# Two key blocks projected in the MLP's accumulation banks, and the first query group's rotations split between VectorE and GpSimd

## The chip, the cores and the metric

The kernel runs on one core of a Trainium2 chip, as one program. The metric is device time in microseconds, lower is better. A core has five engines that run side by side, each through its own list of instructions in order: TensorE (PE in the profile; its weight loads stand apart as PEld), VectorE (DVE), ScalarE (ACT), GpSimd (POOL), and SyncE (SP), which only issues transfers. They wait for one another through semaphores. Matmuls write into PSUM, which has eight banks here, each 128 rows by 512 float32 numbers; the other engines empty the banks.

## The reference

A trunk of two layers on 512 tokens of width 1024, in float32. Layer A is attention and a squared-ReLU MLP. Then keys and values are projected once, for all of layer B, whose attention reads them. Cut to what the change touches:

```python
for layer in range(DEPTH):
    h = rmsnorm(x, attn_norm[layer])
    ...
    else:                                                    # layer B
        k_s, v_s = jnp.split(rmsnorm(x, kv_norm) @ w_kv_shared, 2, axis=-1)
        k_shared = rope(rmsnorm(split_heads(k_s, DIL_SLOTS), kv_k_norm), pos)
        v_shared = split_heads(v_s, DIL_SLOTS)
        q, q_mem = jnp.split(h @ b_w_in[i], [B_Q], axis=-1)
        o_main = dilated_attention(q, k_shared, v_shared, b_q_norm[i])   # q: rmsnorm, rope
        o_mem = memory_attention(...)
        x = x + jnp.concatenate([o_main, o_mem], axis=-1) @ b_w_out[i]
    x = x + squared_relu_mlp(rmsnorm(x, mlp_norm[layer]), w_up[layer], w_down[layer])
```

`rope` turns each pair of halves (x1, x2) of a head into (x1 cos - x2 sin, x1 sin + x2 cos).

## The kernel before, in words

Every float32 product is made from two parts: a number is split into a rounded part and a remainder, and `mm3` (L260, L261, L262) issues three matmuls for each tile: rounded by rounded, rounded by remainder, remainder by rounded. A weight tile is loaded by SyncE into a staging tile `st` (three buffers), ScalarE writes the rounded part into a tile `w` (four buffers, L253), and VectorE or GpSimd subtracts for the remainder (L255; `lo="gv"` takes them by turns).

`proj` multiplies the tokens, in four blocks of 128, with a weight matrix. For each block it takes a bank from `pool` and runs over eight tiles k of the width, so a block has 24 matmuls. `order` is the order of the blocks. The function `evac` then empties the bank. A list as `pool` gives each block, by its number, a pool of its own:

```python
ps = self.ps(pool[b] if isinstance(pool, list) else pool or self.pacc, [P, n])
```

The PSUM pools are `pacc` (2 banks, tiles named `s_acc`), `pS` (3, `s_ps`), `pT` (2, `s_pt`) and `pO` (1, `s_po`).

The place of the first edit is the seam between the first MLP and layer B. The last quarter of the MLP accumulates in banks of all pools; `X` (two banks of `pacc`) and `V` (two of `pT`) are its last. VectorE adds a finished bank into the rows `xn` (L216, in `into`); the function `columns` then transposes 128 x 128 pieces of `xn` by TensorE into `pS` banks (L1251), copies them out (L1258 on ScalarE, L1256 on VectorE) and makes the gained copies (`gained`, L276 on ScalarE and L277 on VectorE) that are the stationary tiles `s_act` of the projections. The tokens of rows 1 (blocks 2 and 3) are ready before those of rows 0 (blocks 0 and 1), and in the last steps `into(X, 0, 0)` comes before the product into `V` has been added.

`layer_b` then projects the keys (`w_kv[0]`, `evac_k`), the values (`w_kv[1]`, `evac_v`), and, sharing TensorE with other work, the queries of four slot groups `sp` (`proj_b`). `evac_k` works on halves of a block: the square sums (`normf`, L505 to L514), a product with the gain that reads the bank (L1419), the rotation (`rope`, L524 to L527, on GpSimd) and a scaling (L1423, GpSimd). `evac_v` scales a block into a tile `raw` (two buffers, L1404) and GpSimd's queue stores it to memory (L1405). `proj_b` empties each block through `normf`, L1466, `rope`, a scaling (L746 in `q_out`), and the split into two parts (`hilo`, L697 on ScalarE, L698 on VectorE), after which TensorE transposes it (L755). `rope` takes its scratch from a tile `rb` with one buffer, whichever engine runs it, and `tq`, which holds the rotated block, has two.

The instructions of each engine are put into an order by a scheduler when the program is built, so an edit can move instructions far from its line. Line numbers after `proj_b`'s edit are two or three higher in the changed kernel (L1466 becomes L1468).

Of the kernel before, what the change touches and what calls it, by code (L numbers as in the profile page):

```python
# [14 lines left out]
P = 128  # L15
# [18 lines left out]
def bcast(ap, dim, n):  # L34

    a = [list(x) for x in ap.ap]
    a.insert(dim, [0, n])
    return bass.AP(tensor=ap.tensor, offset=ap.offset, ap=a)
# [30 lines left out]
def drain(*gens):  # L69
    for g in gens:  # L70
        for _ in g:
            pass
# [7 lines left out]
def weave(main, fill, ratio):  # L80

    due, fill = 0.0, iter(fill)
    for _ in main:
        due += ratio
        while due >= 1.0:
            due -= 1.0
            if next(fill, END) is END:
                due = -1e9
        yield
    yield from fill  # L90
# [51 lines left out]
def attend(items, work, side, ratios, seen, lag=1):  # L142


    late, due = [], 0.0

    def tick(it):
        nonlocal due
        side.step()
        due += ratios[it.seg]  # L150
        while due >= 1.0:
            due -= 1.0
            if work.step() in (END, WAIT):
                due = 0.0

    def back(it):
        it.back(*it.args, it.res)
        tick(it)

    for it in items:  # L160
        if it.need:
            work.need(it.need)
        it.res = it.front(*it.args)
        seen.append(it.seg)
        tick(it)
        late.append(it)
        if len(late) > lag:
            back(late.pop(0))
    for it in late:
        back(it)  # L170
# [10 lines left out]
class K:  # L181
# [1211 lines left out]
    def layer_b(self):  # L1393
        self.ev = 1000000
        nc, ins = self.nc, self.ins
        self.setup_b()
        st = self.rt
        xk = self.xk
        xd = self.xd
        vd = self.dram.tile([S, 512], F32, name="vd")  # L1400

        def evac_v(b, ps):
            t = self.t("raw", [P, 512])
            nc.scalar.activation(t, ps, AF.Copy, scale=st[0][:, b : b + 1])  # L1404
            nc.gpsimd.dma_start(vd[b * P : (b + 1) * P, :], t)  # L1405

        kn = [None] * NB

        gk = self.grow("kk")

        def evac_k(b, ps):
            e = st[1]
            kt = self.t("x", [P, 8, HD])
            kn[b] = kt
            for hf in range(2):
                rw = ps[:, hf * 256 : (hf + 1) * 256]
                f = self.normf(rw, 4, e[:, b])
                kh = kt[:, hf * 4 : hf * 4 + 4]
                nc.vector.tensor_tensor(  # L1419
                    out=kh, in0=rw.rearrange("p (h d) -> p h d", d=HD), in1=bcast(gk[:, 0], 1, 4), op=ALU.mult  # L1420
                )
                self.rope(kh, self.cs[:, b])
                nc.gpsimd.tensor_tensor(out=kh, in0=kh, in1=bcast(f, 2, HD), op=ALU.mult)  # L1423

        drain(self.proj(xk, ins["w_kv"][0], 512, evac_k, pool=self.pS, order=(2, 3, 0, 1)))
        drain(self.proj(xk, ins["w_kv"][1], 512, evac_v, pool=self.pS))
        xg = [self.t("act", [P, 2, S], F32R) for _ in range(KT)]
        for m in range(KT):
            for h in range(2):
                self.gained(xg[m], m, h, "attn1")  # L1430
        e = st[1]
        oT, om, pb, qm, kk = [], [], [[] for _ in range(4)], [], []
        kp, vals = [[] for _ in range(4)], [[] for _ in range(4)]
        work, side, seen = Work(), Work(), []
        for sp in range(1, 4):
            work.add(self.proj_b(sp, xg, e, pb[sp]))
            work.add(self.keys_b(sp, kn, vd, kp[sp]), sp, lambda sp=sp: seen.count(sp - 1) == 8)
        work.add(self.mem_q(1, xg, ins["w_bm"], e, qm))
        work.add(self.mem_keys(1, self.kf1, kk), "mem")
        work.add(self.outpart(oT, 0, 3, ins["w_bo"], xd, 0))  # L1440
        first = weave(self.proj_b(0, xg, e, pb[0], self.pS, DX), self.keys_b(0, kn, vd, kp[0]), WK)
        for i, _ in enumerate(first):
            for _ in range(WB[1] if i >= WB[0] else 0):
                work.step()
        items = []
        for sp in range(4):
            items += self.attn_b(sp, pb[sp], kp[sp], oT, side)
        items += self.mem_items(self.kf1, qm, kk, om, 4, "mem")
        attend(items, work, side, RB, seen)
        while side.step() is not END or work.step() is not END:  # L1450
            pass
        drain(self.outpart(oT + om, 3, 6, ins["w_bo"], None, 3, 3))
# [5 lines left out]
    def proj_b(self, sp, xg, e, res, pool=None, delay=DELAY):  # L1458
        nc, ins = self.nc, self.ins
        q4 = [self.t("qk", [P, 2, S], F32R) for _ in range(3)]  # L1460
        gq = self.grow("bq0", 3)

        def evac(b, ps):
            f = self.normf(ps, 6, e[:, b])
            t = self.t("tq", [P, 6, HD])
            nc.vector.tensor_tensor(  # L1466
                out=t.rearrange("p (g s) d -> p g s d", s=2), in0=ps.rearrange("p (g s d) -> p g s d", s=2, d=HD),
                in1=bcast(gq, 2, 2), op=ALU.mult,  # L1468
            )
            self.rope(t, self.cs[:, b])  # L1470

            def permuted(q):
                d = q.rearrange("p s (r u) -> p s r u", r=4)[:, :, :, 32 * b : 32 * b + 32]
                return lambda pt: nc.scalar.activation(d, pt.rearrange("p s (u r) -> p s r u", r=4), AF.Copy)

            return self.q_out(t, f, [q4[0][:, :, b * P : (b + 1) * P], permuted(q4[1]), permuted(q4[2])])

        yield from self.proj(xg, ins["w_bq"][sp], 384, evac, pool=pool, lo="gv", delay=delay)
        res.extend(q4)
# [326 lines left out]
```

## Time and profile before

| what | value |
|---|---|
| time, median of three runs | 1298.2 us (1295.83 to 1300.5) |
| the profiled execution's own time | 1296.08 us |
| its span from first to last instruction | 1294.3 us |
| TensorE's mean granted clock | 0.995 of full speed |
| TensorE busy | 1244.8 us, 96% of the span |
| VectorE, ScalarE, GpSimd busy | 825.1, 756.5, 379.0 us |

In a row of a timeline stand the start and the length in microseconds, the engine, line and operation, the tile written and the tiles read (buffer numbers left out), the sizes, and how many instructions were merged; brackets hold the engine's idle time before it and what ended that. Times count from the start of the span. The first MLP ends near 683, the keys and values are projected until about 733, and the first query group follows.

### The profile page before, as it was taken

Reading aid. Unit: us, or ns where it says so; the run is one execution under the profiler, and the core shown is the slowest. Engines: PE = TensorE matmul, PEld = TensorE weight load, DVE = VectorE, ACT = ScalarE, POOL = GpSimd, SP = SyncE. Lnnn points to the kernel's source line nnn. Section 1 sums busy time; section 2 is a strip of 40 time slices with the busy share of each in tenths; the row PEclk is TensorE's granted clock in tenths of the full one; section 3 lists DMA queues with packets and bytes.
Section 4 is the critical chain, followed back from the end, with each engine's and each line's share of the span. In section 5 each row is a group of like instructions: output and inputs, shape, how many; then the busy total and the mean of one; then the engine's idle time right before and its main releaser. Section 6 shows DMA issues by size and latency. Waiting matters only on the chain.

```text
span 1294.3 us, 18328 instructions
## 1 busy us (share of the span) xinstructions
PE 1244.8 (96%) x6416; PEld 1021.6 (79%) x6416; DVE 825.1 (64%) x1502; ACT 756.5 (58%) x1684; POOL 379.0 (29%) x478
## 2 busy tenths in 40 slices
PE   9899989899999999999998989998999999999998
PEld 7768777677788888888887888887678888888887
DVE  6846676654656557465588467676657656656566
ACT  6845677774575464554657367777557445355462
POOL 4546665633140010000104689562314000000000
PEclk9999999999999999999999999999999999999999
DMA  7531231334488797887874421210339789697434
GB/s 260 195 119 55 67 126 62 66 74 132 159 252 234 248 238 231 276 237 248 236 212 139 143 74 51 71 42 9 108 126 291 219 271 243 211 287 218 151 110 163
DMA packets 61837, 215.28 MB, mean 166 GB/s; under 512 B 6736, under 2 KB 14928, under 8 KB 61232
## 3 DMA queue, kind: packets, MB, share of 16 engines
q1 hardware_dynamic: 50800, 143.72, 33.7%
q0 software_dynamic: 9344, 35.77, 14.0%
q10 hardware_dynamic: 1600, 34.61, 7.4%
q8 instruction: 51, 0.84, 0.3%
q14 instruction: 42, 0.34, 0.1%
HBM read 208.83 MB, written 72.35 MB: 217 GB/s over the span
## 4 chain that ended last, share of the span: by engine, by line
PE 80%; DVE 8%; ACT 6%; POOL 3%; issue 2%; DMA 2%; POOLq 0%; ACTq 0%; DVEq 0%
PE s_ps L261 14%; PE s_ps L262 13%; PE s_ps L260 13%; PE s_acc L260 5%; PE s_acc L261 5%; PE s_acc L262 5%; PE s_po L734 3%; PE s_pt L261 3%; PE s_pt L262 3%; PE s_pt L260 3%; DVE s_w L255 2%; ACT s_p L216 1%; PE s_ps L1542 1%; PE s_acc L867 1%; PE s_acc L566 1%
## 5 line engine op out<-in xcount | busy, mean ns | idle before, releaser
L255 DVE TENSOR_TENSOR s_w<-s_st,s_w 128x1024 fp32r<-128x1024 f32 (+3 forms) x228 | 272.0, 1197 | 254.7 <-ACT s_w L253 253.7
L253 ACT ACTIVATE s_w<-s_st 128x1024 fp32r<-128x1024 f32 (+4 forms) x260 | 251.3, 970 | 186.8 <-PE s_pt L262 41.1
L260 PE MATMUL s_ps<-s_act,s_w 128*128 128x512 f32 x568 | 222.1, 393 | 1.4 <-ACT s_act L295 1.4
L261 PE MATMUL s_ps<-s_act,s_w 128*128 128x512 f32 x568 | 221.4, 390 | 0.9 <-DVE s_act L1681 0.9
L262 PE MATMUL s_ps<-s_act,s_w 128*128 128x512 f32 x568 | 221.6, 390 | 0.0
L260 PEld LDWEIGHTS s_ps<-s_act,s_w 128*128 128x128 f32 x568 | 106.5, 188 | 25.2 <-ACT s_act L295 3.2
L261 PEld LDWEIGHTS s_ps<-s_act,s_w 128*128 128x128 f32 x568 | 106.7, 188 | 23.3 <-DVE s_act L1681 1.1
L262 PEld LDWEIGHTS s_ps<-s_act,s_w 128*128 128x128 f32 x568 | 106.6, 188 | 21.9
L216 ACT ACTIVATE s_p<-s_ps 128x512 f32<-128x512 f32 x64 | 38.2, 597 | 112.5 <-PE s_ps L262 112.5
L1170 POOL DMA_DIRECT2D sum<-in_w_db_dram x16 | 14.4, 902 | 295.3 <-ACT s_p L216 293.6
L260 PE MATMUL s_acc<-s_w,s_act 128*128 128x512 f32 (+3 forms) x272 | 94.9, 354 | 3.6 <-DVE s_tq L947 2.2
L261 PE MATMUL s_acc<-s_w,s_act 128*128 128x512 f32 (+3 forms) x272 | 95.1, 351 | 2.0 <-POOL s_w L255 1.8
L262 PE MATMUL s_acc<-s_w,s_act 128*128 128x512 f32 (+3 forms) x272 | 93.7, 350 | 0.0
L722 POOL TENSOR_SCALAR s_p<-s_p,s_cr,s_ab 128x128 f32<-128x128 f32 (+3 forms) x96 | 60.3, 664 | 47.9 <-DVE s_cr L1063 26.4
L255 POOL TENSOR_TENSOR s_w<-s_st,s_w 128x512 fp32r<-128x512 f32 (+4 forms) x32 | 54.6, 1706 | 63.6 <-ACT s_w L253 63.5
L216 ACT ACTIVATE s_p<-s_ps,s_nm 128x256 f32<-128x256 f32 (+3 forms) x128 | 65.5, 523 | 9.6 <-DVE s_nm L1043 2.8
L730 ACT ACTIVATE s_pt<-s_pt 128x512 f32<-128x512 f32 (+2 forms) x101 | 52.7, 525 | 20.6 <-PE s_pt L1087 8.5
L295 ACT ACTIVATE s_qk<-s_p 128x256 fp32r<-128x256 f32 (+1 forms) x96 | 47.0, 489 | 22.1 <-DVE s_p L1180 20.1
L260 PEld LDWEIGHTS s_acc<-s_w,s_act 128*128 128x128 f32 x272 | 51.7, 191 | 9.7 <-DVE s_tq L947 1.5
L1170 POOL DMA_DIRECT2D sum<-sum x16 | 14.1, 884 | 147.1 <-DMA sum<-sum 38.4
L261 PEld LDWEIGHTS s_acc<-s_w,s_act 128*128 128x128 f32 x272 | 51.9, 191 | 6.3 <-POOL s_w L255 2.4
L262 PEld LDWEIGHTS s_acc<-s_w,s_act 128*128 128x128 f32 x272 | 51.9, 191 | 3.6
(328 smaller groups left out, 2942.3 us busy)
## 6 DMA issues: line engine op xcount, KB each, us to landing
s_st<-in_w_up_dram SPq DMA_DIRECT2D x64, 512.0 KB, 4.1
s_st<-sum SPq DMA_DIRECT2D x64, 512.0 KB, 6.7
s_st<-in_w_db_dram SPq DMA_DIRECT2D x48, 512.0 KB, 4.5
sum<-in_w_db_dram POOLq DMA_DIRECT2D x16, 1024.0 KB, 13.9
sum<-sum POOLq DMA_DIRECT2D x16, 1024.0 KB, 10.9
s_st<-in_w_bq_dram SPq DMA_DIRECT2D x16, 384.0 KB, 3.1
s_st<-in_w_ag_dram SPq DMA_DIRECT2D x11, 512.0 KB, 3.9
s_w<-in_w_c_dram SPq DMA_DIRECT2D x8, 512.0 KB, 5.0
```

The lines of the kernel that those rows point to most:

```text
L216: return lambda *a, **k: self.marks.append(f(*a, **k))
L253: nc.scalar.activation(w[:, 0], st, AF.Copy)
L255: e.tensor_tensor(out=w[:, 1], in0=st, in1=w[:, 0], op=ALU.subtract)
L260: mm(ps, lh[0], rh[0], start=start, stop=False, skip_group_check=again)
L261: mm(ps, lh[0], rh[1], start=False, stop=False, skip_group_check=again)
L262: mm(ps, lh[1], rh[0], start=False, stop=stop, skip_group_check=again)
L295: nc.scalar.activation(dst[:, 0], src, AF.Copy)
L566: nc.tensor.matmul(banks[b], tiles[k // 4][:, k % 4, b * P : (b + 1) * P], w[:, k % 4 // 2, k % 2 * 512 : k % 2 * 512 + 512], start=k == 0 ...
L722: self.nc.gpsimd.tensor_scalar(out=p, in0=p, scalar1=c, scalar2=g, op0=ALU.mult, op1=ALU.mult)
L730: self.turned = self.nc.scalar.activation(dst, src, AF.Copy)
L734: i = self.nc.tensor.matmul(*a, **k)
L1170: self.behind(self.nc.gpsimd.dma_start(t[o], x, accum_op=ALU.add, max_dma_last_dim=4096))
```

## The change

Two edits. The key projection takes a list of pools: blocks 0 and 1 stay in `pS`, blocks 2 and 3, which come first in `order`, are accumulated in the two `pacc` banks. And in the first query group (`sp == 0`) the rotation and the scaling after it run on VectorE for blocks 0 and 2, on GpSimd for blocks 1 and 3; the other groups keep GpSimd.

```diff
--- before.py
+++ after.py
@@ -1422,7 +1422,9 @@
                 self.rope(kh, self.cs[:, b])
                 nc.gpsimd.tensor_tensor(out=kh, in0=kh, in1=bcast(f, 2, HD), op=ALU.mult)
 
-        drain(self.proj(xk, ins["w_kv"][0], 512, evac_k, pool=self.pS, order=(2, 3, 0, 1)))
+        drain(
+            self.proj(xk, ins["w_kv"][0], 512, evac_k, pool=[self.pS, self.pS, self.pacc, self.pacc], order=(2, 3, 0, 1))
+        )
         drain(self.proj(xk, ins["w_kv"][1], 512, evac_v, pool=self.pS))
         xg = [self.t("act", [P, 2, S], F32R) for _ in range(KT)]
         for m in range(KT):
@@ -1467,13 +1469,14 @@
                 out=t.rearrange("p (g s) d -> p g s d", s=2), in0=ps.rearrange("p (g s d) -> p g s d", s=2, d=HD),
                 in1=bcast(gq, 2, 2), op=ALU.mult,
             )
-            self.rope(t, self.cs[:, b])
+            en = nc.vector if sp == 0 and b % 2 == 0 else nc.gpsimd
+            self.rope(t, self.cs[:, b], en)
 
             def permuted(q):
                 d = q.rearrange("p s (r u) -> p s r u", r=4)[:, :, :, 32 * b : 32 * b + 32]
                 return lambda pt: nc.scalar.activation(d, pt.rearrange("p s (u r) -> p s r u", r=4), AF.Copy)
 
-            return self.q_out(t, f, [q4[0][:, :, b * P : (b + 1) * P], permuted(q4[1]), permuted(q4[2])])
+            return self.q_out(t, f, [q4[0][:, :, b * P : (b + 1) * P], permuted(q4[1]), permuted(q4[2])], e=en)
 
         yield from self.proj(xg, ins["w_bq"][sp], 384, evac, pool=pool, lo="gv", delay=delay)
         res.extend(q4)
```

What the scheduler makes of it, at the places where the order differs most.

TensorE, at the seam, the end of the last transposes and the first key block as it was (`s_ps_6795` is the bank of key block 2; `s_ps_6755` and the like are transposed pieces; `s_pt_1081` here are rows of `xn`):

```order
L1251 MATMUL s_ps_6755<-c_115,s_pt_1081_4072 128x128
L1251 MATMUL s_ps_6755<-c_115,s_pt_1080_4071 128x128
L1251 MATMUL s_ps_6755<-c_115,s_pt_1081_4072 128x128
L260 MATMUL s_ps_6795<-s_w_6787,s_act_6572 128x512
L261 MATMUL s_ps_6795<-s_w_6787,s_act_6572 128x512
L262 MATMUL s_ps_6795<-s_w_6787,s_act_6572 128x512
```

Now the first key matmul, into `s_acc_6795`, stands after two of the sixteen transposes:

```order
L262 MATMUL s_pt_6529<-s_w_6698,s_x_6365 128x512
L1251 MATMUL s_ps_6713<-c_115,s_pt_1080_4071 128x128
L1251 MATMUL s_ps_6725<-c_115,s_pt_1080_4071 128x128
L260 MATMUL s_acc_6795<-s_w_6787,s_act_6572 128x512
L1251 MATMUL s_ps_6713<-c_115,s_pt_1081_4072 128x128
L1251 MATMUL s_ps_6713<-c_115,s_pt_1080_4071 128x128
```

and a little later the second block (`s_acc_6867`, key block 3) begins ahead of the last eight transposes:

```order
L260 MATMUL s_acc_6795<-s_w_6804,s_act_6640 128x512
L260 MATMUL s_acc_6867<-s_w_6787,s_act_6572 128x512
L261 MATMUL s_acc_6867<-s_w_6787,s_act_6572 128x512
L262 MATMUL s_acc_6867<-s_w_6787,s_act_6572 128x512
L1251 MATMUL s_ps_6743<-c_115,s_pt_1080_4071 128x128
```

The 48 matmuls of the two blocks have moved ahead of and between the transposes; the later order of TensorE is nearly the same.

GpSimd, at the end of the keys' rotations (`s_x_7016` is key block 1, `vd` the stored values, `s_raw_7098` and `s_raw_7126` the first two value blocks), the difference:

```order
 L526 TENSOR_TENSOR s_x_7016<-s_x_7016,s_rb_7029 128x4x32
 L527 TENSOR_TENSOR s_x_7016<-s_x_7016,s_rb_7029 128x4x32
+L1405 DMA vd<-s_raw_7098 128x512
 L1423 TENSOR_TENSOR s_x_7016<-s_x_7016,s_r_1563_7025 128x256
 L524 TENSOR_TENSOR s_rb_7047<-s_x_7016,c_115 128x256
-L1405 DMA vd<-s_raw_7098 128x512
+L1405 DMA vd<-s_raw_7126 128x512
 L525 TENSOR_TENSOR s_x_7016<-s_x_7016,c_115 128x256
-L1405 DMA vd<-s_raw_7126 128x512
 L526 TENSOR_TENSOR s_x_7016<-s_x_7016,s_rb_7047 128x4x32
```

The first two value stores have moved ahead by one and two instructions.

VectorE, in the first query group, as it was (`s_tq_7284`, `7339` and `7403` are blocks 0, 1 and 2, `s_qki` their split copies, `s_w_7424` and `s_w_7471` weight tiles of the next group):

```order
L255 TENSOR_TENSOR s_w_7424<-s_st_7422,s_w_7424 128x768
L698 TENSOR_TENSOR s_qki_7292<-s_tq_7284,s_qki_7292 128x6x64
L513 SCALAR_TENSOR_TENSOR s_r_1632_7400<-s_r_1630_7394,et,s_r_1631_7396 128x6
L1466 TENSOR_TENSOR s_tq_7403<-s_ps_7350,gr 128x384
L514 SCALAR_TENSOR_TENSOR s_r_1632_7400<-s_r_1632_7400,s_r_1631_7396 128x6
L255 TENSOR_TENSOR s_w_7471<-s_st_7469,s_w_7471 128x768
```

and now:

```order
L514 SCALAR_TENSOR_TENSOR s_r_1621_7336<-s_r_1621_7336,s_r_1620_7332 128x6
L698 TENSOR_TENSOR s_qki_7292<-s_tq_7284,s_qki_7292 128x6x64
L1468 TENSOR_TENSOR s_tq_7403<-s_ps_7350,gr 128x384
L255 TENSOR_TENSOR s_w_7424<-s_st_7422,s_w_7424 128x768
L513 SCALAR_TENSOR_TENSOR s_r_1632_7400<-s_r_1630_7394,et,s_r_1631_7396 128x6
L514 SCALAR_TENSOR_TENSOR s_r_1632_7400<-s_r_1632_7400,s_r_1631_7396 128x6
L524 TENSOR_TENSOR s_rb_7405<-s_tq_7403,c_115 128x384
L525 TENSOR_TENSOR s_tq_7403<-s_tq_7403,c_115 128x384
L526 TENSOR_TENSOR s_tq_7403<-s_tq_7403,s_rb_7405 128x6x32
L527 TENSOR_TENSOR s_tq_7403<-s_tq_7403,s_rb_7405 128x6x32
L746 TENSOR_TENSOR s_tq_7403<-s_tq_7403,s_r_1632_7400 128x384
L255 TENSOR_TENSOR s_w_7471<-s_st_7469,s_w_7471 128x768
```

The split copy of block 0 (L698) stands ahead of the weight tile 7424 instead of behind it, and five steps of block 2 stand ahead of weight tile 7471. Block 0's own five steps stand a little earlier, between the square sums of blocks 0, 1 and 2.

GpSimd at the same place, block 1's rotation as it was:

```order
L524 TENSOR_TENSOR s_rb_7341<-s_tq_7339,c_115 128x384
L255 TENSOR_TENSOR s_w_7419<-s_st_7417,s_w_7419 128x768
L525 TENSOR_TENSOR s_tq_7339<-s_tq_7339,c_115 128x384
L255 TENSOR_TENSOR s_w_7443<-s_st_7441,s_w_7443 128x768
L526 TENSOR_TENSOR s_tq_7339<-s_tq_7339,s_rb_7341 128x6x32
L527 TENSOR_TENSOR s_tq_7339<-s_tq_7339,s_rb_7341 128x6x32
L746 TENSOR_TENSOR s_tq_7339<-s_tq_7339,s_r_1621_7336 128x384
L524 TENSOR_TENSOR s_rb_7405<-s_tq_7403,c_115 128x384
```

and now:

```order
L1405 DMA vd<-s_raw_7182 128x512
L524 TENSOR_TENSOR s_rb_7341<-s_tq_7339,c_115 128x384
L525 TENSOR_TENSOR s_tq_7339<-s_tq_7339,c_115 128x384
L255 TENSOR_TENSOR s_w_7419<-s_st_7417,s_w_7419 128x768
L526 TENSOR_TENSOR s_tq_7339<-s_tq_7339,s_rb_7341 128x6x32
L527 TENSOR_TENSOR s_tq_7339<-s_tq_7339,s_rb_7341 128x6x32
L255 TENSOR_TENSOR s_w_7443<-s_st_7441,s_w_7443 128x768
L746 TENSOR_TENSOR s_tq_7339<-s_tq_7339,s_r_1621_7336 128x384
```

The rotations of blocks 0 and 2 are gone from it, and one more step of block 1 stands ahead of weight tile 7419.

## The prediction

> **What bounds the kernel now.** I read the page's first block, then busy time by stretches, then TensorE's own timeline for its idle pieces.
>
> ```profile
> PE 1244.8 (96%) x6416; PEld 1021.6 (79%) x6416; DVE 825.1 (64%) x1502; ACT 756.5 (58%) x1684; POOL 379.0 (29%) x478
> ```
>
> ```profile
> 690.00:691.00 1.00, 1.00 (x4) 0.81 (x3) 1.00 (x3) 1.00 (x4) 0.00 (x0) 0.50 0.84 286
> 680.00:690.00 10.00, 6.73 (x33) 5.26 (x32) 9.65 (x19) 9.51 (x20) 0.00 (x0) 0.92 0.82 264
> 690.00:700.00 10.00, 10.00 (x42) 8.21 (x41) 9.58 (x30) 7.39 (x23) 2.68 (x5) 0.91 0.45 163
> 960.00:1260.00 300.00, 300.00 (x1341) 248.67 (x1340) 184.46 (x269) 161.76 (x240) 22.27 (x20) 1.00 0.75 220
> ```
>
> The columns are the stretch, its length, busy time of TensorE, of its weight loads, of VectorE, ScalarE and GpSimd, then TensorE's granted clock and the DMA. TensorE is the bound. From 960 to 1260 it is busy 300 of 300 us, so what is gained before is carried to the end. Only its idle pieces can pay, and the change touches the stretch from 680 to 780. Two groups of pieces lie there: one at the seam between the MLP and layer B, one in the first query group.
>
> ```profile
> 682.89 1.03 PE L1251 MATMUL s_ps<-c,s_pt 128*128 128x128 f32 x8
> 685.66 0.33 PE L1251 MATMUL s_ps<-c,s_pt 128*128 128x128 f32 x1 [1.74 <-DVE s_pt L216]
> 687.19 0.33 PE L1251 MATMUL s_ps<-c,s_pt 128*128 128x128 f32 x1 [1.19 <-ACT s_x L1258]
> 687.85 1.07 PE L1251 MATMUL s_ps<-c,s_pt 128*128 128x128 f32 x6 [0.34 <-DVE s_pt L216]
> 688.57 0.78 PE L260 MATMUL s_ps<-s_w,s_act 128*128 128x512 f32 x1
> 691.99 0.39 PE L262 MATMUL s_ps<-s_w,s_act 128*128 128x512 f32 x1
> ```
>
> Columns: start, length, instruction, and in brackets the idle time before it and what ended it. At the seam TensorE idles 1.74 + 1.19 + 0.34 = 3.27 us, and then the clock is 0.50: eight matmuls take 688.57 to 691.99, 3.42 us.
>
> ```profile
> 737.55 0.44 PE L261 MATMUL s_ps<-s_w,s_act 128*128 128x384 f32 x1 [1.23 <-DVE s_w L255]
> 751.87 0.51 PE L260 MATMUL s_acc<-s_w,s_act 128*128 128x384 f32 x2
> 754.72 0.70 PE L755 MATMUL s_pt<-idr,s_qki 128*128 128x128 f32 x6 [2.34 <-DVE s_qki L698]
> 770.96 0.68 PE L755 MATMUL s_pt<-idr,s_qki 128*128 128x128 f32 x6 [1.53 <-DVE s_qki L698]
> ```
>
> In the query groups the largest piece, 2.34 us, waits for the first rotated block (L698 follows its rotation).
>
> **Edit 1: key blocks 2 and 3 in the MLP's banks.** No work is added; 48 matmuls move ahead of, and between, the last transposes. What they need:
>
> ```profile
> 677.64 0.75 DVE L216 SCALAR_TENSOR_TENSOR s_pt<-s_acc,r,s_pt 128x512 f32<-128x512 f32 x1
> 680.23 0.75 DVE L216 SCALAR_TENSOR_TENSOR s_pt<-s_acc,r,s_pt 128x512 f32<-128x512 f32 x1
> 685.92 1.22 DVE L255 TENSOR_TENSOR s_w<-s_st,s_w 128x1024 fp32r<-128x1024 f32 x1
> 688.31 1.22 DVE L255 TENSOR_TENSOR s_w<-s_st,s_w 128x1024 fp32r<-128x1024 f32 x1
> 695.82 0.39 ACT L505 ACTIVATE s_sq<-s_ps 128x256 f32<-128x256 f32 x1 [0.98 <-PE s_ps L262]
> 701.26 0.39 ACT L505 ACTIVATE s_sq<-s_ps 128x256 f32<-128x256 f32 x1 [2.00 <-PE s_ps L262]
> ```
>
> The banks are free at 680.98. A key block takes 701.26 - 695.82 = 5.44 us, 0.227 a matmul. From 682.89 sixteen transposes (two times 1.03) and two blocks (10.88) end at 695.83; with 0.2 for the signal, ScalarE sees block 3 done at 696.0 instead of 701.26: 5.2 earlier. Counted the other way: 3.27 idle, and 3.42 - 8 x 0.227 = 1.6 of half clock, 4.9. I take 5.0. The third weight tile is ready at 687.14 and wanted near 689.6, the fourth at 689.53 and wanted near 691.4, so neither stalls it. Bounds: 0 (something I miss holds the blocks) to 5.2. One weight load on SP's queue passes one store; its consumer is the value projection, more than two blocks away, so that costs nothing.
>
> **What gives part of it back.** The keys' rotations stay on GpSimd, and the first waits for VectorE, which is busy 9.58 of 10 us from 690 to 700 with work that does not move. So GpSimd still starts at 697.09:
>
> ```profile
> 697.09 0.73 POOL L524 TENSOR_TENSOR s_rb<-s_x,c 128x256 f32<-128x256 f32 x1 [51.58 <-DVE s_r L228]
> 722.11 0.46 POOL L527 TENSOR_TENSOR s_x<-s_x,s_rb 128x128 f32<-128x128 f32 x1
> 726.78 0.62 POOL L1423 TENSOR_TENSOR s_x<-s_x,s_r 128x256 f32<-128x256 f32 x1
> 731.68 1.84 POOL L255 TENSOR_TENSOR s_w<-s_st,s_w 128x768 fp32r<-128x768 f32 x1 [1.61 <-ACT s_w L253]
> 728.51 0.69 ACT L1404 ACTIVATE s_raw<-s_ps,rt 128x512 f32<-128x512 f32 x1 [4.32 <-PE s_ps L262]
> 730.75 0.83 ACT L253 ACTIVATE s_w<-s_st 128x768 fp32r<-128x768 f32 x1
> vd<-s_raw POOLq DMA_DIRECT2D x4, 256.0 KB, 2.4
> ```
>
> Its rotations run without a pause to 727.4. In the new order the first value store (L1405) stands behind the L527 that ends at 722.57; its landing takes 2.4, so 725.0. (The store passes one rotation step and one scaling, which holds ScalarE's first key rounding up by 0.6, while nothing waits for it.) The third value eviction (L1404, 728.51) reuses that store's source buffer and can now start at 725.0 to 725.4, 3.1 to 3.5 earlier, not 5.0. Behind it on ScalarE stand the gained copies and the first query weight (L253, ends 731.58), and behind that GpSimd's L255 (731.68 to 733.52), which also needs the rotations and a store ended. It would run near 728.3 to 730.1. TensorE comes for it near 728.6 and waits some 1.6. Of 5.0 about 3.3 is left; bounds 2.5 and 5.0. The 1.23 at 737.55 hangs on VectorE behind the same copies and moves along unchanged.
>
> **Edit 2: rotations of blocks 0 and 2 on VectorE.** Ten instructions leave GpSimd and come to VectorE.
>
> ```profile
> L524 DVE TENSOR_TENSOR s_rb<-s_tq,c x2: 549/554/558, 33.8 to 44.1; 128x384 f32<-128x384 f32 x2
> 744.92 0.55 DVE L1466 TENSOR_TENSOR s_tq<-s_ps,gr 128x384 f32<-128x384 f32 x1
> 748.84 0.54 DVE L507 TENSOR_REDUCE s_r<-s_sq 128x6 f32<-128x384 f32 x1
> 750.87 2.53 DVE L255 TENSOR_TENSOR s_w<-s_st,s_w 128x768 fp32r<-128x768 f32 x1 [1.49 <-ACT s_w L253]
> 753.32 1.34 DVE L698 TENSOR_TENSOR s_qki<-s_tq,s_qki 128x384 fp32r<-128x384 f32 x1
> 748.97 0.83 POOL L746 TENSOR_TENSOR s_tq<-s_tq,s_r 128x384 f32<-128x384 f32 x1
> 750.74 1.84 POOL L255 TENSOR_TENSOR s_w<-s_st,s_w 128x768 fp32r<-128x768 f32 x1
> 752.55 1.70 POOL L525 TENSOR_TENSOR s_tq<-s_tq,c 128x384 f32<-128x384 f32 x1
> ```
>
> Times here are of the old run, before any shift. A rotation costs VectorE 3 x 0.55 and two halves, 0.3 each as an estimate: 2.25. Block 0's first four fit into its pauses between 745.5 and 748.4; L746 comes after the reduction at 748.84, so 749.4 to 749.9. ScalarE's rounding and L698, now ahead of the weight subtraction (2.53) that it stood behind, end near 751.1. TensorE is free for its transposes at 754.72 - 2.34 = 752.38: the 2.34 goes. GpSimd's L255 for the next weights follows two instructions of block 1, which wait for the one scratch tile (rb) until 748.4; it ends near 752.4, and TensorE asks at 752.9. Block 2 on VectorE waits for the same scratch until GpSimd's L527 of block 1, near 753.5. Queued behind it are the last weight subtraction (L255), a cast and the next roundings. It ends 755.8, or 757.5 if its steps stretch as L698 did (1.34); that L255 then ends by 758.6. TensorE asks for it near 759.3 (36 matmuls of 0.17, three quarters of the key's 0.227, after 752.9, and two transposes), so 0.7 of cover. Edit 2: -2.3, bounds 0 and -3.9 (the 1.53 at 770.96 too, which I leave: its block stays with GpSimd).
>
> **Sum.** -3.3 - 2.3 = -5.6. The profiled execution took 1296.1, 1.8 more than its span, and would take 1290.5; the runs' median is 2.1 above it, so 1292.6.
>
> [...] GpSimd's L525 took 1.70 beside VectorE's work and L698 1.34. [...]
>
> The clock. The 0.50 at 690 follows pieces of which none is above 1.74. [...]
>
> **Rivals.**
> A: GpSimd does not hold the query weights back, because stores land sooner or its rotations start earlier. -5.0 - 2.3 = -7.3, with 770.96 gone -8.8. Against it: the 9.58 of 10.
> [...]
> C: the clock drops once more, 3.42 us at half, +1.6: -4.0.
> D, slower: VectorE, in order, stands at block 2's scratch while its L255 and the next reductions wait. Every microsecond past the 0.7 of cover is TensorE's. To lose 3.9 net, GpSimd would have to come 5.6 + 3.9 + 0.7 = 10.2 late with the five instructions up to that L527. With all five at 1.84 it takes 9.2 instead of the 5.1 above (748.4 to 753.5): 4.1 late.
>
> **Numbers.** A measurement of this kernel can tell about 0.3%, 3.9 us. Forecast (-4.5 to -6.8) 0.50, A 0.14, B 0.18, C 0.12, D 0.06. Faster: the forecast, A, a third of B, over a third of C, 0.74; same 0.20; slower 0.06. The range runs from A's 1289.4 to B's 1294.9, widened by the spread of the runs (1295.83 to 1300.5, some 2.3 each way): 1287 to 1297.2.
>
> **What would show it.** Right: no idle piece above 0.3 between 682.9 and 695; granted clock 1.00 there; ScalarE's L505 for block 3 near 696 or as soon as it is free; GpSimd's first L524 still near 697; a new TensorE wait of 1 to 2 us on GpSimd's L255 near 728 to 730; no wait at the first L755; VectorE idle before its second L524, released by GpSimd. Wrong: key matmuls that stall on weights or inputs at 685 to 691; the half clock found elsewhere; a wait on GpSimd's or VectorE's L255 near 747 to 754 in place of the 2.34; or the attention after 785 giving the lead back: it is not all TensorE's, as this stretch shows.
>
> ```profile
> 840.00:860.00 20.00, 17.53 (x141) 16.57 (x141) 15.75 (x33) 15.54 (x47) 17.95 (x19) 1.00 0.26 74
> ```
>
> There 2.47 of 20 us are idle; I let them move along whole, since what ends them follows TensorE's own results.

## The result, and the profile after

The changed kernel took 1290.07 us (median of 13 runs, 1286.46 to 1295.03), the kernel before 1298.18 us beside it (13 runs): ratio 0.9946, 95% interval 0.9929 to 0.9963. A repetition gave 1289.98 against 1296.38 us, ratio 0.9943 (0.9922 to 0.9963). So 8.1 and 6.4 us are gained by the medians, 7.0 and 7.4 by the ratios. 1292.6 was forecast, from 1287.0 to 1297.2. The profiled execution of after took 1287.75 us, its span 1285.7.

The first block of the page and the same stretches as before (stretch, length, busy time of TensorE, weight loads, VectorE, ScalarE, GpSimd; then granted clock and DMA):

```profile
PE 1243.1 (97%) x6416; PEld 1021.4 (79%) x6416; DVE 829.2 (64%) x1512; ACT 756.1 (59%) x1684; POOL 369.3 (29%) x468
...
690.00:691.00 1.00, 1.00 (x7) 0.82 (x6) 1.00 (x4) 1.00 (x4) 0.00 (x0) 1.00 1.00 368
680.00:690.00 10.00, 10.00 (x54) 8.25 (x53) 9.59 (x19) 9.55 (x20) 0.00 (x0) 1.00 0.80 256
690.00:700.00 10.00, 10.00 (x46) 8.29 (x45) 9.90 (x32) 8.34 (x27) 2.68 (x5) 1.00 0.47 169
```

TensorE no longer idles between 680 and 700 (10.00 of 10 us busy in both stretches), and the clock there is 1.00. Its timeline at the seam shows the transposes (L1251) with key matmuls between them and no idle time in brackets:

```profile
682.32 0.38 PE L1251 MATMUL s_ps<-c,s_pt 128*128 128x128 f32 x2
682.45 0.48 PE L260 MATMUL s_acc<-s_w,s_act 128*128 128x512 f32 x1
682.77 0.82 PE L1251 MATMUL s_ps<-c,s_pt 128*128 128x128 f32 x6
...
686.88 0.27 PE L1251 MATMUL s_ps<-c,s_pt 128*128 128x128 f32 x1
```

Behind the seam, the rows that the prediction named (timelines of GpSimd, ScalarE and TensorE):

```profile
697.08 0.73 POOL L524 TENSOR_TENSOR s_rb<-s_x,c 128x256 f32<-128x256 f32 x1 [52.19 <-DVE s_r L229]
728.01 1.82 POOL L255 TENSOR_TENSOR s_w<-s_st,s_w 128x768 fp32r<-128x768 f32 x1
```

```profile
698.40 0.37 ACT L505 ACTIVATE s_sq<-s_acc 128x256 f32<-128x256 f32 x1
724.79 0.69 ACT L1404 ACTIVATE s_raw<-s_ps,rt 128x512 f32<-128x512 f32 x1 [0.88 <-DMA vd<-s_raw]
```

```profile
729.89 0.44 PE L261 MATMUL s_ps<-s_w,s_act 128*128 128x384 f32 x1 [1.41 <-POOL s_w L255]
746.91 0.63 PE L755 MATMUL s_pt<-idr,s_qki 128*128 128x128 f32 x6
754.95 0.44 PE L261 MATMUL s_acc<-s_w,s_act 128*128 128x384 f32 x1 [0.57 <-DVE s_w L255]
764.65 0.67 PE L755 MATMUL s_pt<-idr,s_qki 128*128 128x128 f32 x6 [1.87 <-DVE s_qki L698]
```

GpSimd starts its key rotations at the old time, 697.08. The third value eviction waits 0.88 for a store's landing, and TensorE then waits 1.41 for GpSimd's L255. The first L755 (746.91) no longer waits. But a wait of 0.57 on VectorE's last weight subtraction and one of 1.87 at the fourth L755 have come (the fourth L755 had 1.53 before). The subtraction stands behind block 2's first rotation step, which took 2.19 beside GpSimd's L255 (VectorE, then GpSimd):

```profile
749.47 2.19 DVE L524 TENSOR_TENSOR s_rb<-s_tq,c 128x384 f32<-128x384 f32 x1
```

```profile
749.40 1.85 POOL L255 TENSOR_TENSOR s_w<-s_st,s_w 128x768 fp32r<-128x768 f32 x1
```

Behind the 1.87 the clock is at half, 0.50 from 766 to 768:

```profile
764.00:766.00 2.00, 1.19 (x9) 1.08 (x10) 1.43 (x4) 0.81 (x4) 1.84 (x4) 0.97 0.00 0
766.00:768.00 2.00, 2.00 (x8) 2.00 (x7) 0.66 (x2) 1.33 (x5) 1.38 (x2) 0.50 0.00 0
```

To see where the gain arises I compare the start of the same TensorE instruction in two timelines. The table gives start in the kernel named minus start in before; a change between two columns is what that stretch gave (down) or cost (up). The first column holds differences from the kernel's start, which no edit touches.

| kernel | 672 | 701 | 741 | 798 | 871 | 962 |
|---|---|---|---|---|---|---|
| after | -0.57 | -5.99 | -5.31 | -4.39 | -4.56 | -8.62 |
| after, repeated (e11) | -2.44 | -7.86 | -8.01 | -7.31 | -4.64 | -7.09 |
| edit 1 alone (e1) | -1.15 | -6.56 | -6.37 | -4.92 | -4.94 | -9.04 |
| edit 2 alone (e2) | -1.99 | -1.75 | -1.73 | -0.10 | +2.60 | +3.29 |
| before, new late order (e7) | -0.88 | -0.49 | -0.46 | +3.64 | +13.76 | +9.60 |
| edit 1, old late order (e8) | -1.06 | -6.47 | -6.03 | -4.48 | +3.10 | +4.30 |

After gains 5.4 at the seam, where 5.0 was forecast; holds 3.8 of it at 798 (4.39 - 0.57); and then gains 4.1 more between 871 and 962, where the prediction had nothing. There TensorE's order differs: the build's scheduler has moved the memory attention's score matmuls (L657) ahead of a part of the output projection. A piece of TensorE's order there (+ in after, - in before, from row 3935 on). Rows of this order merge repeated instructions; rows 3300 to 3800, which come up below, run in before from about 821 to 863 us where they were changed, rows 3800 to 4080 from 882 to 945.

```
 L262 MATMUL s_acc_9578<-s_act_9352,s_w_9575 128x512
-L644 MATMUL s_pt_9470<-idr,s_qki_9467 128x128 x4
-L1591 MATMUL s_pt_9508<-c_115,s_p_2079_9414 128x128 x2
+L1594 MATMUL s_pt_9508<-c_115,s_p_2079_9414 128x128 x2
+L657 MATMUL s_ps_9487<-s_qk_9450,s_qk_9024 128x256
+L657 MATMUL s_ps_9544<-s_qk_9450,s_qk_9024 128x256
+L657 MATMUL s_ps_9612<-s_qk_9450,s_qk_9024 128x256
...
 L260 MATMUL s_acc_9636<-s_act_8302,s_w_9633 128x512
```

Between the last two marks of the table TensorE idles 7.65 us in before and 5.21 in after. Its idle pieces from 925 to 950, first of before, then of after:

```profile
931.31 0.50 PE L1669 MATMUL s_pt<-s_p,s_ab 8*128 8x512 f32 x1 [0.69 <-DVE s_p L1665]
932.68 0.50 PE L1674 MATMUL s_pt<-s_p,s_ab 8*128 8x512 f32 x1 [0.87 <-ACT s_pt L730]
940.20 0.50 PE L261 MATMUL s_ps<-s_act,s_w 128*128 128x512 f32 x1 [0.91 <-DVE s_act L1681]
946.46 0.74 PE L260 MATMUL s_ps<-s_act,s_w 128*128 128x512 f32 x2 [0.70 <-ACT s_act L295]
```

```profile
930.50 0.70 PE L260 MATMUL s_ps<-s_act,s_w 128*128 128x512 f32 x2 [1.66 <-DVE s_act L1683]
932.12 0.73 PE L261 MATMUL s_ps<-s_act,s_w 128*128 128x512 f32 x2 [0.58 <-DVE s_act L1684]
```

### The profile page after: what moved, and what is told of

Same layout as the page of the kernel before. It is cut to its first block, busy times and chain, and to the rows that moved or that the text cites. A ratio compares the mean times of both kernels' runs of the same rounds, so it can differ in the third digit from the quotient of the medians.

```text
span 1285.7 us, 18330 instructions
## 1 busy us (share of the span) xinstructions
PE 1243.1 (97%) x6416; PEld 1021.4 (79%) x6416; DVE 829.2 (64%) x1512; ACT 756.1 (59%) x1684; POOL 369.3 (29%) x468
## 4 chain that ended last, share of the span: by engine, by line
PE 76%; DVE 8%; ACT 5%; POOL 4%; DMA 3%; issue 2%; SPq 0%; POOLq 0%; ACTq 0%; DVEq 0%
PE s_ps L261 13%; PE s_ps L262 13%; PE s_ps L260 13%; PE s_acc L260 5%; PE s_acc L261 5%; PE s_acc L262 5%; PE s_pt L260 3%; PE s_pt L261 3%; PE s_pt L262 3%; PE s_po L734 3%; ACT s_p L216 1%; DVE s_w L255 1%; PE s_ps L1545 1%; PE s_acc L867 1%; PE s_acc L566 1%
## 5 line engine op out<-in xcount | busy, mean ns | idle before, releaser
L255 DVE TENSOR_TENSOR s_w<-s_st,s_w 128x1024 fp32r<-128x1024 f32 (+3 forms) x228 | 269.0, 1184 | 255.7 <-ACT s_w L253 254.6
L260 PE MATMUL s_acc<-s_w,s_act 128*128 128x512 f32 (+3 forms) x288 | 102.0, 360 | 4.3 <-DVE s_tq L947 1.6
L261 PE MATMUL s_acc<-s_w,s_act 128*128 128x512 f32 (+3 forms) x288 | 102.1, 356 | 1.6 <-POOL s_w L255 0.9
L262 PE MATMUL s_acc<-s_w,s_act 128*128 128x512 f32 (+3 forms) x288 | 100.5, 355 | 0.0
L255 POOL TENSOR_TENSOR s_w<-s_st,s_w 128x512 fp32r<-128x512 f32 (+4 forms) x32 | 56.0, 1750 | 52.1 <-ACT s_w L253 52.1
L260 PEld LDWEIGHTS s_acc<-s_w,s_act 128*128 128x128 f32 x288 | 55.4, 193 | 11.3 <-ACT s_w L253 1.9
L261 PEld LDWEIGHTS s_acc<-s_w,s_act 128*128 128x128 f32 x288 | 55.5, 193 | 6.5 <-POOL s_w L255 1.3
L262 PEld LDWEIGHTS s_acc<-s_w,s_act 128*128 128x128 f32 x288 | 55.4, 193 | 4.2
```

What stands on the lines that cost most here:

```text
L255: e.tensor_tensor(out=w[:, 1], in0=st, in1=w[:, 0], op=ALU.subtract)
L260: mm(ps, lh[0], rh[0], start=start, stop=False, skip_group_check=again)
L261: mm(ps, lh[0], rh[1], start=False, stop=False, skip_group_check=again)
L262: mm(ps, lh[1], rh[0], start=False, stop=stop, skip_group_check=again)
```

## The experiments

Ratios are to the kernel before in runs on the same chip.

| kernel | median, us (runs) | before (runs) | ratio, 95% interval |
|---|---|---|---|
| e1 edit 1 alone | 1288.68 (10) | 1296.32 (27) | 0.9938 (0.9916 to 0.9960) |
| e2 edit 2 alone | 1298.45 (11) | 1296.32 | 1.0007 (0.9992 to 1.0022) |
| e5 four key blocks in `pacc` | 1296.48 (11) | 1296.32 | 1.0005 (0.9987 to 1.0023) |
| e4 block 3 on VectorE too | 1286.66 (6) | 1296.32 | 0.9933 (0.9909 to 0.9956) |
| e7 before, new late order | 1300.18 (12) | 1296.28 (32) | 1.0024 (0.9999 to 1.0048) |
| e8 edit 1, old late order | 1299.65 (12) | 1296.28 | 1.0015 (0.9990 to 1.0040) |
| e6 second group's first block | 1288.42 (9) | 1296.28 | 0.9928 (0.9903 to 0.9954) |
| e3 no landing wait | 1295.37 (10) | 1296.28 | 0.9981 (0.9959 to 1.0004) |
| e11 after, repeated | 1289.98 (8) | 1296.38 (20) | 0.9943 (0.9922 to 0.9963) |
| e9 wait filled | 1291.66 (10) | 1296.38 | 0.9958 (0.9937 to 0.9979) |
| e10 block 0 alone | 1289.66 (9) | 1296.38 | 0.9944 (0.9924 to 0.9965) |

**The edits apart.** e1 is the pool list of the diff without the rotations' engine; e2 the reverse.

> Key blocks 2 and 3 in the MLP's banks, rotations of the first query group all on GpSimd as before. The schedule shows two places changed against before: the seam, and TensorE's order in the last stretch of attention (rows 3800 to 4080, 137 of 280 rows stand elsewhere). Theory 1 (the trace of after): the seam gives 5.4, about 0.7 of it is given back near 728, the new order at 895 to 946 gives another 3 to 4; against before -7 to -9, in the trace one microsecond or less idle between 900 and 950 beside 4.56 before. Theory 2 (the prediction): only the seam pays, -3.3, and the stretch at 895 to 946 moves along whole. In both the 2.34 at the first L755 of the query group stands.

> Keys in the old banks, rotations of query blocks 0 and 2 on VectorE. The schedule differs from before only in the first query group. Theory 1: the 2.34 goes, but block 3, still on GpSimd, and VectorE's last weight subtraction bring 0.3 to 1 of new idle each; idle of 740 to 790 falls from 5.34 to about 4.1, so -1.2; if a half-clock window falls behind the wait on block 3 as it did in after, +0.5. Theory 2 (the prediction): -2.3. The seam keeps its 3.27 idle, and the stretch at 895 to 946 its 4.56.

e1 is as fast as after (-7.6 us) and e2 as slow as before (+2.1 by the medians; by its ratio's interval -1.0 to +2.9). Theory 1 holds for e1: -5.41 at the seam, and -4.1 between 871 and 962. Its 2.34 stands (2.33), and the trace shows half a clock behind it, from 748.58 to 751.99. e2 has lost the 2.34 and has the new waits (TensorE's timelines of e1, then of e2):

```profile
748.34 0.96 PE L755 MATMUL s_pt<-idr,s_qki 128*128 128x128 f32 x6 [2.33 <-DVE s_qki L698]
```

```profile
758.54 0.44 PE L261 MATMUL s_acc<-s_w,s_act 128*128 128x384 f32 x1 [0.54 <-DVE s_w L255]
768.23 0.72 PE L755 MATMUL s_pt<-idr,s_qki 128*128 128x128 f32 x6 [1.87 <-DVE s_qki L698]
```

**The late order by itself.** Is the gain between 871 and 962 due to the order, or to coming there earlier? A harmless repetition moves the order: VectorE copies the second group's keys of block 3 once more (before, e7) or three times more (edit 1 alone, e8) to the same place.

```diff
+            for _ in range(1 if (sp, c) == (1, 3) else 0):      # e8: 3
+                nc.vector.tensor_copy(d[0], pt.rearrange("p s (u r) -> p s r u", r=4))
             self.keys_out(pt.rearrange("p s (u r) -> p s r u", r=4), *d)
```

> Before, with one copy of the second group's keys (block 3) done twice by VectorE (0.4 us, off TensorE's path); both edits are absent. That moves the schedule: the seam's rows stand as in before, rows 3300 to 3800 of TensorE's order differ in 115 places, and rows 3800 to 4080 stand word for word as in after. Theory 1, that order alone is worth some 4: -3 to -4.5 against before, idle from 890 to 950 near 3.6 instead of 5.65, the seam's 3.27 unchanged. Theory 2, the stretch pays only because TensorE comes to it 5 earlier: within 1 of before.

> Edit 1 alone, with the same copy done four times (1.2 us of VectorE): the seam's rows stand as in after, rows 3300 to 3800 nearly as in the kernel of the run above (8 differ), and rows 3800 to 4080 word for word as in before. Theory 1: -3.5 to -4.5 against before, 4 short of edit 1 alone; lead at 880 about 4, at 950 no more than that. Theory 2: -7 to -8.5, as edit 1 alone.

Both times are missed by both theories (e7 +3.9, e8 +3.4 against before), and neither kernel decides alone, since both pay for a third thing between 798 and 871, where rows 3300 to 3800 stand and which I had expected to be neutral: e7 loses 10.1 there, e8 7.6. e7 has lost 4.1 before that, between 741 and 798, to three half-clock windows (from 755.9, 772.9 and 786.6), though TensorE's order there is row for row that of before. Together they do decide, if the third thing costs the same in both. With a for the seam, b for the late order, m for the middle, and adding them up: a + b = -7.6 (e1), m + b = +3.9 (e7), a + m = +3.4 (e8), so m = 7.4, b = -3.5, a = -4.1, each uncertain by some 2.6. If the late order were worth nothing, e8 would be at 3.9 - 7.6 = -3.7; it is at +3.4.

The places say the same of b, without that condition. From 871 to 962 every profile with the new order (or with two rows of it elsewhere) gains: after 4.1, e1 4.1, e3 4.1, e6 4.3, e7 4.2, e11 2.5, e10 2.0, e9 1.8. With the old one e2 and e8 lose 0.7 and 1.2; e4 and e5, whose order is neither, lose 0.7 and 0.5. Profiles with as much half clock in this stretch can be compared: with one window it took 86.7 to 87.0 us in the new order (after, e1, e6) and 91.0 in the old (before); with two, 86.9 to 89.1 (e3, e7, e10, e11) and 91.7 (e2); with two and a half, 89.2 (e9) and 92.2 (e8). So theory 1: the late order is worth 2.6 to 4.8, also where the seam is the old one (e7).

What m is stays open in part. Most of it is half clock, not idle time: from 798 to 871 TensorE idles only 1.5 (e7) and 2.3 (e8) longer than in before, but six windows of half clock stand there in e7 and three and a half in e8, none in before. And this stretch varies without any new order: of the profiles that run it in the order of before, after gains 0.2 there, and e11, e3 and e9 lose 2.7, 2.7 and 5.4. In the runs the mean granted clock was 0.989 (e7) and 0.990 (e8), 0.992 in before and 0.994 in e1. Why the changed rows fall into half clock more often is not shown.

**The seam's banks.** e5 puts all four key blocks into `pacc`.

```diff
-pool=[self.pS, self.pS, self.pacc, self.pacc]
+pool=[self.pacc, self.pacc, self.pacc, self.pacc]
```

> After, with all four key blocks in the two MLP banks. TensorE's order at the seam and in the first query group is that of after row for row; its order in rows 3800 to 4080 is not (128 of 280 rows stand elsewhere; 55 differ from before). Theory 1, the order of the last stretch is worth 3 to 4: 1292 to 1294, 2 to 4 above after, with idle from 890 to 950 near 4.5. Theory 2, that order is worth nothing and after's lead there was chance: within 1 of after.

Its time, 1296.48, is above what either theory said, and it doesn't answer its question, since TensorE's order at the seam is not all: block 0 now waits until VectorE has emptied block 2.

```profile
697.90 0.47 PE L260 MATMUL s_acc<-s_w,s_act 128*128 128x512 f32 x1 [2.56 <-DVE s_r L513]
```

With the half clock at 698.7 the seam's lead is 1.0 instead of 5.4. So blocks 0 and 1 need banks of their own: in e5 VectorE, which in after is busy 9.90 of 10 us there, had read block 2's bank to the end only at 697.8 (L1419, the row before the L513 of the bracket).

**The value store.** e3 evicts the values into another pool (`self.t("p2", [P, 512])` for `raw` in `evac_v`).

> After, with the four value blocks evicted into a pool with six free buffers, so that the third (L1404) no longer waits for the first store to land. TensorE's, VectorE's and SP's order are those of after. Theory 1, GpSimd's own row of rotations (from 697.09 without a pause to 727.4, then L255 at 728.01) is what TensorE waits for at 729.89: L1404 starts up to 0.9 earlier, TensorE's wait stays within 0.3 of 1.41, total within 1 of after. Theory 2 (the prediction's step), the landing holds the weights up: the wait falls to 0.5, -0.9.

The landing wait is gone, and ScalarE is through with its copies sooner. Theory 1 holds for the first wait (1.36). But a second wait appears (in e3 TensorE, then GpSimd, then VectorE; last VectorE in after):

```profile
727.99 0.44 PE L261 MATMUL s_ps<-s_w,s_act 128*128 128x384 f32 x1 [1.36 <-POOL s_w L255]
...
731.93 0.44 PE L261 MATMUL s_ps<-s_w,s_act 128*128 128x384 f32 x1 [1.59 <-DVE s_w L255]
```

```profile
726.11 3.82 POOL L255 TENSOR_TENSOR s_w<-s_st,s_w 128x768 fp32r<-128x768 f32 x2
```

```profile
722.99 8.02 DVE L277 SCALAR_TENSOR_TENSOR s_act<-s_x,gv,s_act 128x256 fp32r<-128x256 f32 x8 [0.51 <-ACT s_act L276]
730.93 1.96 DVE L255 TENSOR_TENSOR s_w<-s_st,s_w 128x768 fp32r<-128x768 f32 x2
```

```profile
725.91 5.41 DVE L277 SCALAR_TENSOR_TENSOR s_act<-s_x,gv,s_act 128x256 fp32r<-128x256 f32 x8 [1.50 <-ACT s_act L276]
```

GpSimd's two subtractions now run back to back beside VectorE's eight L277, which take 8.02 instead of 5.41; VectorE's L255 behind them is late. The lead between 701 and 741 falls by 2.0 (7.58 to 5.60), where after's falls by 0.7. That wait explains some 1.5 of the 4 to 5 by which e3 is slower than after. Its runs had a mean granted clock of 0.9905, those of after 0.993, which is some 3 us of lost clock in 1290; why e3 meets more half clock stays open. Neither theory had this: in after only the first of GpSimd's two ran beside the eight, where one L277 took 1.89 (the median is 0.48), and the second started at 730.95, when the last of them had begun.

**Edit 2's new wait.** e4, e6 and e10 choose other blocks for VectorE: `sp == 0 and b != 1`; `(sp, b) in ((0, 0), (0, 2), (1, 0))`; `(sp, b) in ((0, 0),)`.

> After, with block 3's rotation on VectorE too (only block 1 of the first query group stays on GpSimd). Theory 1: the 1.87 that TensorE waits for block 3's L698 at 764.65 hangs on GpSimd's rotation (757.74 to 761.97, 4.2 for the five steps; VectorE has 2.25 and pauses of 1.24 and more there): it falls below 0.5 and the half clock behind it at 766 goes: -1.4 to -3 against after. Theory 2: block 3 waits for TensorE's and ScalarE's own steps (statistics on ScalarE until 762.7), so it stays above 1.2: within 0.7 of after. The order at 900 to 946 differs from after's in 25 rows, which can hide 1 of it.

> After, with the rotation of the second query group's first block on VectorE as well. Theory 1: TensorE's 1.87 at 764.65 waits for this block (its product lies in an MLP bank; GpSimd rotates it from 757.74 to 761.97, then ScalarE's rounding and VectorE's L698 at 763.95). VectorE does the five steps in 2.6 where GpSimd takes 4.2: the wait falls to 0.5 or less, and no half-clock window follows it; lead over before at 785 rises from 4.4 to 6 to 8. Theory 2: VectorE's queue (statistics and products of three blocks at 757 to 764) holds the steps up as much, and more than 1.2 is left. From 785 on the order differs in many rows (394 of 500), so the end time is not the test; 1284 to 1292.

> After, with block 2's rotation back on GpSimd, so that VectorE rotates block 0 alone. Theory 1, block 0 is what removes the 2.34 and block 2 brings the new wait for VectorE's last weight subtraction (its first rotation step stood 2.19 beside GpSimd): the 2.34 stays away, the 0.57 near 755 goes, the wait for the second group's first block stays above 1.2; idle from 740 to 790 3.5 to 4.2, time within 1.5 of after. Theory 2, block 2 then comes late from GpSimd and TensorE waits for it near 761: idle from 740 to 790 above 4.8, 1 to 2 above after.

The expectation of e4 named the wrong block: the tile numbers in TensorE's order show that this fourth L755 transposes the second group's first block. So e6 moves that one. In all three the wait stays (TensorE's timelines of e4, e6 and e10; last VectorE's of e6):

```profile
762.46 0.68 PE L755 MATMUL s_pt<-idr,s_qki 128*128 128x128 f32 x6 [1.70 <-DVE s_qki L698]
```

```profile
767.07 0.67 PE L755 MATMUL s_pt<-idr,s_qki 128*128 128x128 f32 x6 [1.84 <-DVE s_qki L698]
```

```profile
765.58 0.93 PE L755 MATMUL s_pt<-idr,s_qki 128*128 128x128 f32 x6 [2.48 <-DVE s_qki L698]
```

```profile
763.08 0.94 DVE L514 SCALAR_TENSOR_TENSOR s_r<-s_r,s_r 128x6 f32<-128x6 f32 x1
...
764.55 0.97 DVE L746 TENSOR_TENSOR s_tq<-s_tq,s_r 128x384 f32<-128x384 f32 x1
```

e4 moved another block, so it says nothing of this wait. In e6 theory 2 holds: with the rotation on VectorE, over at 762.9, the scaling L746 still waits for the statistics (L513, L514) and for what stands between. ScalarE had the input of L513 ready at 761.75 (L511), but L513 stood behind the rotation's own last steps in VectorE's queue and started at 762.83:

```profile
761.54 0.21 ACT L511 ACTIVATE s_r<-s_r 128x6 f32<-128x6 f32 x1
```

```profile
762.83 0.22 DVE L513 SCALAR_TENSOR_TENSOR s_r<-s_r,et,s_r 128x6 f32<-128x6 f32 x1
```

So the block comes as late by VectorE's queue as it did by GpSimd's. In e10 the 0.57 is gone, as theory 1 said, but TensorE waits 2.48: its idle pieces from 740 to 790 add up to 3.98, in after to 4.15. All three times lie within each other's intervals and e1's; none of these versions can be told from edit 1 alone.

**The half clock.** e9 fills the wait at 764.65 in after; all other orders are after's.

```diff
                 pt = self.ps(self.pT, [P, n, P])
+                for _ in range(warm if j == 0 else 0):      # 6 for (sp, b) == (1, 0)
+                    nc.tensor.matmul(pt.rearrange("p a b -> p (a b)"), self.idr, fill, start=True, stop=True)
```

> After, unchanged, beside the two kernels below. The start of the half-clock windows lies on a grid of 3.4133 us in each profile so far, at another phase each time; so this profile should keep the idle pieces of the first one within 0.1 (1.4 near 730, 1.9 near 765) and show its half-clock windows at other places. Time: -6 to -9 against before.

> After, with six matmuls (idr by an activation tile, 128x512, 0.23 us each) into the PSUM tile of the transposes that wait at 764.65, ahead of these; what they write is overwritten by the transposes. Every engine's order is that of after but for the six. Theory 1: a half-clock window follows that wait (five of six profiles that have it) because TensorE is busy for only 1.4 to 1.75 of the 3.41 us before; with 1.4 more of work in the wait it does not come; the matmuls take the place of idle time, so they cost nothing: idle there falls from 1.87 to about 0.5, lead at 785 is 1.0 to 1.7 more than after's, and the time -0.5 to -1.7 against after. Theory 2: the clock asks for useful matmuls or for longer work, the window comes all the same, and the time is after's or 0.5 more.

In e9 the six matmuls take the place of idle time, and no half clock follows before 777.1 (TensorE's timeline):

```profile
761.70 1.56 PE L755 MATMUL s_pt<-s_act,idr 128*128 128x512 f32 x6
763.63 0.70 PE L757 MATMUL s_pt<-idr,s_qki 128*128 128x128 f32 x6 [0.36 <-DVE s_qki L698]
```

But it need not follow without them either: in e11 it came only at 775.1, and in e6, with its wait of 1.84, there was none at all from 290 to 896. And e9 has eight such windows in all, one at 777.1. The idle time went as theory 1 said (0.36 left). The lead did not last: over after it was 0.9 at 755, ahead of the six matmuls, 2.5 at 770, and 1.1 at 782, behind e9's own half clock at 777.1. Nor does the time hold: e9 cannot be told from after. So e9 shows that the wait can be filled at no cost, and not that this keeps the clock. e11 kept the 1.87, as expected, but its wait near 730 was 0.82, not 1.4; its time, -6.4, is in the range.

## Why the prediction was right, and where not

The total is right, but by luck: two errors of opposite sign, edit 2's 2.3 that did not come and 4.1 that nobody forecast, leave it inside its range. The gain of 6.4 to 8.1 is nearer to rival A's 7.3 than to the forecast's 5.6, but A's reason did not come: GpSimd started at its old time and did hold TensorE up. The steps:

- The seam: +5.0 forecast, 5.4 measured in each of the nine profiles that have blocks 2 and 3 alone in `pacc`. No idle piece, clock 1.00, GpSimd's start at 697.08: right. Block 3's squares were to start near 696 or as soon as ScalarE is free; they started at 698.40.
- What gives part back: a wait of 1.6 on GpSimd's L255 near 728.6 forecast, 1.41 at 729.89 in after, 1.15 in e1, 0.82 in e11. The landing (third L1404 at 725.0 to 725.4 forecast, 724.79 measured) and L255 (728.3 forecast, 728.01 measured) came as worked out. Two things failed: the landing is not what TensorE waits for, GpSimd's own row is (e3); and the 1.23 at 737.55, which was to move along, went, so that only 0.7 was given back by 741 instead of 1.7.
- The half clock: the 1.6 was not kept. It came again at 765.9 in after and at 748.5 in e1, 3.41 us at half each time: the drop that rival C had. At 798 e1 keeps 5.41 - 0.18 - 1.45 = 3.8 of edit 1; 3.3 was forecast.
- Edit 2: -2.3 forecast, nothing to be told from zero measured (e2; after and e11 beside e1). The step that failed is that the cover holds behind the first L755. The 2.34 did go; 0.57 came on VectorE's L255, where 0.7 of cover was reckoned (its block 2 stood 2.19 in one step), and 1.87 on a block that the forecast left at 1.53. The idle pieces from 740 to 790 fell by 1.2 (5.34 to 4.15), and in after a half clock behind the 1.87 cost as much. That it pays nothing, B's 1294.9, was right in its size, but as the author's estimate: no run shows TensorE held by GpSimd's L255 in place of the 2.34; in after and e2 it waited for VectorE's L255 (0.57 and 0.54) and L698 (1.87 in both).
- "I let them move along whole": wrong. I had read the scheduler's order at the two edits alone; edit 1 changes it 200 us later too, and that gave the 4.1.

Sum as measured: 3.8 + 0 + 4.1 = 7.9 less, against 8.1 by the medians and 5.6 forecast. That it meets 8.1 so closely is chance too: the repetition's medians gave 6.4, and its profile 2.5 in the last stretch in place of 4.1, with one half-clock window more.

## What to carry to other kernels

Where a scheduler sets the order, compare the whole order, not the edited places: here the order 200 us behind the edit was worth 4.1 us, as much as the edit with its 3.8. Before an engine is relieved of work, ask what its block waits for next: the engine that takes the work over can hold the block's next step in its own queue for as long (a wait of 1.84 in e6, of 1.87 in after). A small change should be read against the granted clock of its runs, which moved single runs here by more than the edits did (8.9 us between the runs of before with a high and a low clock, in the section below). And a wait may be worth keeping: without the landing wait both of GpSimd's L255 ran beside VectorE's eight L277, these took 8.02 us instead of 5.41, and TensorE had a second wait, of 1.59 (e3).

## What the runs showed of the hardware

In the trace's record of the granted clock the half-clock windows start on a grid: in before at 183.483, 698.896 and 944.655 us of that record, which are 151 and 72 times 3.4133 apart; in after at 182.364, 776.283 and 905.989, which are 174 and 38 times. Most last 3.413 us, the longer ones two or five times that (two in e8 from 848.6, five in e7 from 830.9). The grid stands at another phase in each profile: its first line after 150 us of the span is at 151.43 in after, 152.55 in before and 150.53 in e11. It is such a window that the prediction needed, and not the length of one piece of idle time (1.87 was followed by half a clock in after, and 1.87 in e11 was not): in these traces the half clock goes with how busy TensorE was in one window of the grid. The rows of four such windows (stretch, length, TensorE's busy time, clock, DMA), of after, of e11 and of e9:

```profile
728.29:731.70 3.41, 2.00 (x12) 1.00 0.43 157
762.42:765.83 3.41, 1.38 (x11) 1.00 0.00 0
```

```profile
771.75:775.16 3.41, 1.83 (x13) 1.00 0.38 115
```

```profile
760.09:763.51 3.42, 3.17 (x20) 1.00 0.00 0
```

Behind the second and third follows half a clock, behind the others not. I counted the windows between 150 and 1280 us that ran at full clock, over all 13 profiles: of 37 in which TensorE was busy for less than 1.9 us, 32 were followed by half a clock; of 246 with 1.9 to 2.75, 37; of those with more, none. An exact threshold was not found. Of the 37 in this second group, 22 held matmuls of 8 rows (the 8x512 above), of the other 209 only 8 did; whether such matmuls count for less was not tested. Once at half clock, work alone did not always end it: in e7 the half clock stayed for 17 us (830.9 to 848), five windows, though TensorE was busy for 3.2 to 3.4 us of each.

The same program had another number of windows in each of its two profiles, with the grid at another phase: after had three between 150 and 1280 us in one (span 1285.7), four in the other (1287.2), and e9, after with filled idle time, eight (1292.4): 1.5 and 1.3 us for each window more. The granted clock of each run says the same of the spread: of the 79 runs of before beside the experiments, the 17 with a clock of 0.995 or more have a median of 1294.3 us, the 13 with less than 0.990 one of 1303.2. So a wait in a profile has no fixed price: the 1.84 of e6 cost itself, the 1.87 of after some 1.5 more.
